# Two first parts on ScalarE before two second parts on VectorE, x's splits off GpSimd, and a new order in the fourth block

## The chip, the core and the metric

The kernel runs on one core of a Trainium2 chip. TensorE multiplies 128x128 tiles into PSUM; VectorE (DVE in the profile), ScalarE (ACT) and GpSimd (POOL) work on tiles of 128 partitions; SyncE (SP) issues the transfers to and from HBM. Each engine runs its own queue in order and waits on semaphores for the others. The metric is device time in microseconds (us); the median of the runs counts.

## The reference

One layer of a streaming encoder, for a prompt of 1024 frames and a second group of 64 new frames with caches. The part in which most of the change lies is the first projection and the two attentions behind it:

```python
h  = rms_norm(x, g_norm1)
p  = h @ w_in                       # q, k, v of 8 heads "A" and 8 heads "B", and forget logits
q, k = rms_norm(q, g_q), rms_norm(k, g_k)       # per head, 64 numbers
A: each chunk of 64 frames attends to itself and 8 chunks before, with a relative-position bias
B: causal attention, logit[t, s] += sum of log sigmoid(forget logit) over s < j <= t
x += concat(o_A, o_B) @ w_o
x += memory cross-attention (256 memory tokens, 4 heads);  x += ConvFFN(x)
```

## The kernel before, in words

**Split numbers.** TensorE multiplies in a rounded 32-bit format. For more exact results each operand is held as two parts: the first part is the operand rounded to that format, the second part is what rounding left. A product is then three matmuls (first x first, second x first, first x second: the names `hi` and `lo`). The split of x, `split_x` (L126), writes `xhi` on GpSimd for odd k and on ScalarE for even k (k counts eight slices of 128 of the 1024 model columns), then `xlo` on VectorE. The split of turned queries and keys, `gained` (L254), writes the first part on ScalarE and then the second on VectorE.

**The first stage** (0 to about 574 us) goes over eight pairs of heads, p = 0 to 7, and for each over eight blocks of 128 frames, t = 0 to 7, and the 64 new frames. A block's projection is 24 matmuls into a PSUM tile `pj` (two buffers). `proj` (L292) copies the result out on ScalarE (`qkraw`, `sq`, `vf`), and gives back two functions that are woven between the matmuls of later blocks:

- `norm`: the norms of queries and keys. VectorE sums and adds (`m`), splits the values (`v`); GpSimd takes the power (`r`) and scales (`qk`, `ko`).
- `turn`: TensorE transposes the four `qk` tiles into one PSUM bank `tq` (one buffer), and `gained` splits them twice: keys into `kh` and `kl`, queries into the two halves of `q`. The next block's transposes can't start before the bank has been read.

Scores then go to a PSUM tile `S` (one buffer), are read by VectorE (`mx`), put through the exponential on ScalarE, scaled on GpSimd, transposed (`PT`) and multiplied by the values (`O`).

**What pair 0 has besides.** In the first pair x itself must be split, 256 columns at a time (`columns(c, z)`: column group c, half z of the eight slices; c = 4 is the 64 new frames, in a tile `xs`), and its norms taken (`norms`: a square with a sum over each 128 rows on ScalarE, then `stats_end`). `early` says which of this work goes to which block, ahead of or behind the attention pieces of the block. `substeps(slow)` puts those pieces in a row: norms of the last block (`ns`), transposes held from the block before (`first`), scores, values. Blocks 0 and 1 of pair 0 are multiplied together; block 2 comes third, block 3 fourth.

**What sets the order.** The Python order is where a compile-time scheduler starts; it puts each engine's queue in an order by its own estimate of when things are ready. `in_order` pins part of it (the splits of x among it). So an edit in one place can move instructions elsewhere.

**The stage after** prepares keys and values of the memory: `load_mem` splits its 1024x256 input (`memT` into `mhi`, `mlo`, also with `gained`), `split_wm` the weights (`mwraw` into `mwhi`, `mwlo`), while the last attention pieces of the first stage are still running.

Of the kernel before, what the change touches and what calls it, by code (L numbers as in the profile page):

```python
# [9 lines left out]
ACT = mybir.ActivationFunctionType  # L10
ALU = mybir.AluOpType
# [30 lines left out]
def hybrid_step(ctx: ExitStack, tc: tile.TileContext, i: dict, o: dict):  # L42
# [3 lines left out]
    def f32(ap):  # L46
        return ap.bitcast(F32)
# [75 lines left out]
        e.tensor_tensor(lo[:, :nw], raw[:, :nw], f32(hi[:, :nw]), op=ALU.subtract)  # L123
        return hi, lo

    def split_x(hi, lo, raw, k):  # L126
        if k % 2:
            pool.tensor_scalar(hi, raw, gcol[:, 0, k:k + 1], 1.0, op0=ALU.mult, op1=ALU.mult)
        else:
            act.activation(hi, raw, ACT.Copy, scale=gcol[:, 0, k:k + 1])  # L130
        dve.scalar_tensor_tensor(lo, raw, gcol[:, 0, k:k + 1], f32(hi), op0=ALU.mult, op1=ALU.subtract)  # L131
# [40 lines left out]

    def split_col(c, k, raw):
        dst = [xs[:, k, a] for a in range(2)] if c == 4 else [a[:, k, c * 256:(c + 1) * 256] for a in x2]
        split_x(*dst, raw[:, k % 4], k)

    def columns(c, z, raw=None):
        raw = raw or load_x(c, z)
# [72 lines left out]
                           gk[:rows, kind:kind + 1].broadcast_to([rows, 2, 64]), op=ALU.mult)  # L251
        return qk, ko.rearrange("p h d -> p (h d)")

    def gained(hi, lo, src, g, rows=slice(0, P)):  # L254

        act.activation(hi, src, ACT.Copy, scale=g)
        dve.scalar_tensor_tensor(lo, src[rows], g[rows], f32(hi[rows]), op0=ALU.mult, op1=ALU.subtract)
# [34 lines left out]
    def proj(p, t, pj):  # L292

        g = groups.get((p, t // 2)) or Group()
        groups[p, t // 2] = g
        j = t % 2
        raw = wa.tile([P, 256], F32, name="qkraw", bufs=2)
        act.copy(raw, pj[:, 0:256])
        sq = squares(pj[:, 0:256], P)
        vf = wa.tile([P, 2, 64], F32, name="vf", bufs=2)  # L300
        act.activation(vf.rearrange("p h d -> p (h d)"), pj[:, 256:384], ACT.Copy, scale=rstd1[:, t:t + 1])
        if p == 0:
            dve.scalar_tensor_tensor(flog[:, t], pj[:, 384:392], rstd1[:, t:t + 1], bfb, op0=ALU.mult, op1=ALU.add)
        qk = kflat = None

        def norm():
            nonlocal qk, kflat
            qk, kflat = qk_norm(p, sq, raw, eps1[:, t:t + 1], P)
            dve.tensor_copy(g.v[:, j, :, 0], vf)
            dve.tensor_tensor(g.v[:, j, :, 1], vf, f32(g.v[:, j, :, 0]), op=ALU.subtract)  # L310

        def turn():
            tq = bank("tq").rearrange("p (a b) -> p a b", a=4)
            for h in range(4):
                pe.transpose(tq[:, h], qk[:, h].rearrange("p a d -> p (a d)"), ident)
            c = slice(j * P, j * P + P)
            kind = p // 4
            gained(g.kh[:, :, c], g.kl[:, :, c], tq[:, 2:4], gd[:, kind, 1:2])
            gained(g.q[:, :, c], g.q[64:, :, c], tq[:, 0:2], gd[:, kind, 0:1], slice(64, P))
            vflat = vf.rearrange("p h d -> p (h d)")  # L320
            cols = slice((p % 4) * P, (p % 4) * P + P)
            if p >= 4:
                nc.sync.dma_start(o["bk"][t * P:(t + 1) * P, cols], kflat)
                nc.sync.dma_start(o["bv"][t * P:(t + 1) * P, cols], vflat)
            elif t >= 4:
                nc.sync.dma_start(o["ak"][(t - 4) * P:(t - 3) * P, cols], kflat)
                nc.sync.dma_start(o["av"][(t - 4) * P:(t - 3) * P, cols], vflat)

        return norm, turn
# [229 lines left out]
    def substeps(slow=False):  # L559

        sc = todo[0].scores() if todo else []
        va = late.pop(0).values() if late else []
        if todo:
            late.append(todo.pop(0))
        ns, ts = [x for x, _ in turns], [x for _, x in turns]
        turns.clear()
        first = held[:]
        held[:] = ts if slow else []
        r = ns + first + sc[:1] + ends if slow else first + sc[:1] + ends + ns
        r += va[:1] + sc[1:] + va[1:-1] + ([] if slow else ts)  # L570
        ends[:] = va[-1:]
        return [f for f in r if f]
# [4 lines left out]
    def scale_gain():  # L577
# [1 line left out]

    early = {1: lambda: (norms(0, 1) + columns(1, 0, xraws[2]), []),  # L580
             2: lambda: (columns(1, 1, xraws[3]), [scale_gain] + norms(2, 3) + columns(2, 0, xraws[4]) + [lambda: load_bias(0)]),
             3: lambda: (columns(2, 1, xraws[5]), norms(4, 5)), 4: lambda: ([], columns(3, 0)), 5: lambda: ([], columns(3, 1) + norms(6)),
             6: lambda: ([], norms(7, 8) + columns(4, 0) + columns(4, 1))}
    forgetting = []
    for p, np_ in zip(PAIRS, PAIRS[1:] + (None,)):
# [56 lines left out]
    def load_mem(z):  # L642
        raw = wk.tile([P, N], F32, name="s", bufs=4)[:, :1024].rearrange("p (k t) -> p k t", k=4)
        nc.sync.dma_start(raw, i["memT"][4 * z:4 * z + 4].rearrange("k p t -> p k t"))
        for k in range(4):
            gained(mem[0][:, 4 * z + k], mem[1][:, 4 * z + k], raw[:, k], gcol[:, 3, 4 * z + k:4 * z + k + 1])

    def load_wm(n, z):
        raw = mp.tile([P, 4, 256], F32, name="mwraw", bufs=2)
# [54 lines left out]
    class Sample:  # L704
# [31 lines left out]
        def prep(self):  # L736
# [6 lines left out]
                pe.transpose(tq[:, x, :S], self.qd[:, x], ident[:S, :S])  # L743
            self.q = mq.tile([P, 2, S], F32R, name="sq_", bufs=2)
            self.kn = [mq.tile([P, 2, S], F32R, name=f"skn{x}", bufs=2) for x in range(2)]
            gained(self.q, self.q[64:], tq[:, 0:2, :S], gd[:, p // 4, 0:1], slice(64, P))
            gained(self.kn[0], self.kn[1], tq[:, 2:4, :S], gd[:, p // 4, 1:2])
            if p >= 4:
                b = self.s
                pool.tensor_scalar(b, b, stok[:, p - 4:p - 3], 1.0, op0=ALU.add, op1=ALU.mult)  # L750
# [1099 lines left out]
```

## Time and profile before

| | |
|---|---|
| median of 3 runs (lowest to highest) | 1797.08 us (1796.71 to 1797.51) |
| the profiled execution: its own time | 1797.27 us |
| its span in the trace | 1795.2 us |
| busy in the span: TensorE, VectorE, ScalarE, GpSimd | 1716.4, 1224.5, 930.2, 664.1 us |
| mean load of the DMA engines, 0 to 45 us and over the span | 0.76; 111 GB/s |

A row of a timeline reads: start in us, duration in us, engine, line, operation, output <- inputs, shape, how many alike in a row, and in brackets the idle time before it with what ended it. Matmuls overlap, so their durations are longer than their distance. A row of the waits reads: who waited, for whom, total us, how many times, the longest. A row of the windows reads: stretch, its length, then busy us of TensorE, its weight loads, VectorE, ScalarE and GpSimd with counts, then the granted TensorE clock, the DMA load and GB/s.

### The profile page before, as it was taken

The page shows a single profiled execution, that of the slowest core. Times are in us where ns is not written, and L with a number is a line of the kernel's source. Part 1 is how long each engine was busy: PE and PEld are TensorE (multiplying, and loading weights), DVE is VectorE, ACT ScalarE, POOL GpSimd, SP SyncE. Part 2 cuts the span into 40 slices and gives each one's busy share as a digit, 9 for nine tenths or more (in the row PEclk, how much of TensorE's full clock was granted, in tenths as well). Part 3 has the DMA queues.
Part 4 walks back from the last instruction along what each step waited for, and adds up shares of the span by engine and source line. Part 5 has one row for each costly group of instructions (what it writes and reads, how often), then busy time and mean ns, then how long its engine had stood idle before and what let it go on. Part 6 is the DMA issues. An engine that isn't in the chain of part 4 may idle for free. (4 is left out here: it accounts for less than half of the span.)

```text
span 1795.2 us, 34082 instructions
## 1 busy us (share of the span) xinstructions
PE 1716.4 (96%) x12432; PEld 1664.3 (93%) x12432; DVE 1224.5 (68%) x2710; ACT 930.2 (52%) x2042; POOL 664.1 (37%) x1025
## 2 busy tenths in 40 slices
PE   6898999999998888999999999999999999999999
PEld 5788999999997777999999999999999999999999
DVE  5778667677677797433444379877777777677994
ACT  5656667677677577433555455433333333434332
POOL 5656657779777554443444521100000000000000
PEclk8999999999999999999999999999999999999999
DMA  7322222122112776542111563222222222794232
GB/s 244 93 68 57 62 75 72 55 72 76 47 59 79 221 246 216 164 137 65 54 54 60 149 216 103 78 79 74 87 83 89 73 73 72 254 312 157 77 118 80
DMA packets 134248, 199.87 MB, mean 111 GB/s; under 512 B 20968, under 2 KB 74088, under 8 KB 134080
## 3 DMA queue, kind: packets, MB, share of 16 engines
q1 hardware_dynamic: 134080, 197.70, 34.8%
q8 instruction: 98, 1.61, 0.4%
q14 instruction: 70, 0.57, 0.1%
HBM read 155.35 MB, written 45.44 MB: 112 GB/s over the span
## 5 line engine op out<-in xcount | busy, mean ns | idle before, releaser
L288 PE MATMUL pj<-whi,xhi 128*128 128x384 f32 (+1 forms) x512 | 194.9, 381 | 3.4 <-ACT xhi L130 1.7
L288 PE MATMUL pj<-wlo,xhi 128*128 128x384 f32 (+1 forms) x512 | 176.1, 344 | 3.4 <-POOL wlo L123 3.4
L288 PE MATMUL pj<-whi,xlo 128*128 128x384 f32 (+1 forms) x512 | 174.7, 341 | 0.7 <-DVE xlo L131 0.7
L1540 POOL COPY s<-gp 128x2 f32<-128x2 f32 x22 | 15.8, 719 | 335.8 <-DVE gp L1539 335.8
L1434 PE MATMUL W<-h,hi 128*128 128x272 f32 x704 | 134.4, 288 | 1.4 <-ACT qlo L1570 1.4
L493 ACT ACTIVATE s<-s,mx 128x640 f32<-128x640 f32 (+7 forms) x128 | 94.4, 737 | 75.0 <-DVE mx L491 74.1
L1731 PE MATMUL W<-f,hi 128*128 128x272 f32 x672 | 127.7, 288 | 3.5 <-DVE f L1299 1.7
L530 DVE TENSOR_TENSOR ptl<-PT,pth 128x512 fp32r<-128x512 f32 (+2 forms) x192 | 99.5, 522 | 39.1 <-ACT pth L529 37.0
L1434 PEld LDWEIGHTS W<-h,hi 128*128 128x128 f32 x704 | 110.8, 188 | 1.7 <-ACT qlo L1570 1.6
L1731 PEld LDWEIGHTS W<-f,hi 128*128 128x128 f32 x672 | 105.3, 188 | 4.4 <-DVE gp L1505 2.4
L243 POOL TENSOR_TENSOR r<-m,mhalf 128x4 f32<-128x4 f32 (+1 forms) x72 | 73.9, 1027 | 92.4 <-DVE m L242 90.0
L529 ACT CAST pth<-PT 128x512 fp32r<-128x512 f32 (+2 forms) x192 | 85.0, 448 | 39.5 <-PE PT L528 37.9
L288 PEld LDWEIGHTS pj<-whi,xhi 128*128 128x128 f32 x512 | 98.9, 193 | 5.2 <-ACT xhi L130 2.3
L288 PEld LDWEIGHTS pj<-wlo,xhi 128*128 128x128 f32 x512 | 98.7, 193 | 5.3 <-POOL wlo L123 5.1
L1434 PE MATMUL W<-h,lo 128*128 128x272 f32 x352 | 101.8, 289 | 0.0
L1298 ACT CAST hi<-raw 128x512 fp32r<-128x512 f32 x68 | 42.2, 621 | 109.1 <-PE W L1434 59.1
L288 PEld LDWEIGHTS pj<-whi,xlo 128*128 128x128 f32 x512 | 97.3, 190 | 1.4 <-DVE xlo L131 1.2
L1731 PE MATMUL W<-f,lo 128*128 128x272 f32 x336 | 96.7, 288 | 0.0
L528 PE MATMUL PT<-ident,s 128*128 128x128 f32 x528 | 89.7, 277 | 6.2 <-DVE ptl L530 5.4
L246 POOL TENSOR_SCALAR qk<-qkraw,r 128x128 f32<-128x128 f32 x256 | 91.5, 375 | 5.9
L488 PE MATMUL S<-kh,q 128*128 128x256 f32 (+1 forms) x304 | 77.4, 280 | 12.8 <-DVE mx L491 12.7
L922 PE MATMUL pj<-a,hi 128*128 128x384 f32 (+1 forms) x352 | 89.5, 337 | 0.0
(606 smaller groups left out, 6051.3 us busy)
## 6 DMA issues: line engine op xcount, KB each, us to landing
raw<-in_w_down_dram SPq DMA_DIRECT2D x45, 256.0 KB, 2.9
wraw<-in_w_dram SPq DMA_DIRECT2D x56, 192.0 KB, 2.4
raw<-in_w_up_dram SPq DMA_DIRECT2D x41, 256.0 KB, 2.8
h<-ad SPq DMA_DIRECT2D x32, 272.0 KB, 4.7
mwraw<-in_w_mkv_dram SPq DMA_DIRECT2D x16, 512.0 KB, 5.2
raw<-in_w_mo_dram SPq DMA_DIRECT2D x32, 256.0 KB, 3.3
kvraw<-in_w_down_dram SPq DMA_DIRECT2D x32, 256.0 KB, 3.3
ad<-t SPq DMA_DIRECT2D x22, 272.0 KB, 2.1
```

The source lines that it names most:

```text
L243: pool.tensor_tensor(r[:rows], m[:rows], mhalf[:rows, 0:4], op=ALU.pow)
L246: pool.tensor_scalar(qk[:rows, h], raw[:rows, h * 64:(h + 1) * 64].rearrange("p (o d) -> p o d", o=1).broadcast_to([rows, 2, 64]), r[:rows ...
L288: pe.matmul(pj[:, :nw], x2[a][:, k, t * P:(t + 1) * P], wt[k][b][:, :nw], start=n == 0, stop=n == 3 * KT - 1)
L488: pe.matmul(sp[:, a:a + (k1 - k0) * P], q, kk[:, h, src], start=m == 0, stop=m == 1)
L493: act.activation(s[:, :n], s[:, :n], ACT.Exp, bias=mx, scale=-1.0, accum_out=sm)
L528: pe.transpose(pt[:, b - ch[0]], self.s[j][:, (b - w0) * P:(b - w0 + 1) * P], ident)
L529: act.copy(hi[:, f:f + n, j], pt[:, f:f + n])
L530: dve.tensor_tensor(lo[:, f:f + n, j], pt[:, f:f + n], f32(hi[:, f:f + n, j]), op=ALU.subtract)
L922: pe.matmul(out()[:, :cn], w[a][:, k % 4], x[b][k][:, c0:c0 + cn], start=k == 0 and n == 0, stop=k == KT - 1 and n == 2)
L1298: act.copy(hi, t)
L1434: pe.matmul(w[:, z, :Q], a(p, j), rights[j][b][:, z * Q:z * Q + Q], start=fresh and begin and j == 0 and x == 0, stop=final and end and j ...
L1731: pe.matmul(ws[m][:, z, :Q], la[p][:, m * P:(m + 1) * P], ra[b][:, z * Q:z * Q + Q], start=first and y == 0 and what in opening, stop=fina ...
```

## The change

```diff
-    def split_x(hi, lo, raw, k):
-        if k % 2:
+    def split_x(hi, lo, raw, k, first):
+        if k % 2 and first:
             pool.tensor_scalar(hi, raw, gcol[:, 0, k:k + 1], 1.0, op0=ALU.mult, op1=ALU.mult)
         else:
             act.activation(hi, raw, ACT.Copy, scale=gcol[:, 0, k:k + 1])
...
-        split_x(*dst, raw[:, k % 4], k)
+        split_x(*dst, raw[:, k % 4], k, c == 0)
...
-    def gained(hi, lo, src, g, rows=slice(0, P)):
-
-        act.activation(hi, src, ACT.Copy, scale=g)
-        dve.scalar_tensor_tensor(lo, src[rows], g[rows], f32(hi[rows]), op0=ALU.mult, op1=ALU.subtract)
+    def gained(*items):
+
+        for hi, lo, src, g, rows in items:
+            act.activation(hi, src, ACT.Copy, scale=g)
+        for hi, lo, src, g, rows in items:
+            dve.scalar_tensor_tensor(lo, src[rows], g[rows], f32(hi[rows]), op0=ALU.mult, op1=ALU.subtract)
...
-            gained(g.kh[:, :, c], g.kl[:, :, c], tq[:, 2:4], gd[:, kind, 1:2])
-            gained(g.q[:, :, c], g.q[64:, :, c], tq[:, 0:2], gd[:, kind, 0:1], slice(64, P))
+            gained((g.kh[:, :, c], g.kl[:, :, c], tq[:, 2:4], gd[:, kind, 1:2], ALL),
+                   (g.q[:, :, c], g.q[64:, :, c], tq[:, 0:2], gd[:, kind, 0:1], LOWER))
...
-        r = ns + first + sc[:1] + ends if slow else first + sc[:1] + ends + ns
+        r = first[:1] + ns + first[1:] + sc[:1] + ends if slow else first + sc[:1] + ends + ns
...
-             3: lambda: (columns(2, 1, xraws[5]), norms(4, 5)), 4: lambda: ([], columns(3, 0)), 5: lambda: ([], columns(3, 1) + norms(6)),
+             3: lambda: (columns(2, 1, xraws[5]) + norms(4, 5), []), 4: lambda: ([], columns(3, 0)), 5: lambda: ([], columns(3, 1) + norms(6)),
...
-                subs = ahead + subs + behind
+                subs = subs[:t == 3] + ahead + subs[t == 3:] + behind
```

It has four parts. `gained` takes both splits of one bank together (also for the new frames later; `load_mem` still calls it with one). The first parts of x are written by ScalarE except in column group 0. In blocks 2 to 6 of pair 0 the oldest held transposes go ahead of the norms. In the fourth block (t = 3) these transposes go ahead of the split of x, and the norms of x for blocks 4 and 5 come right behind that split instead of at the block's end. Behind `gained` the lines are numbered 4 higher.

**Fourth block, VectorE.** Before, from the logits of block 2 to the reduction of the first score (`m`, `v` are the norm of block 2; the two pairs `kl`, `q` are the transposes of blocks 0 and 1):

```order
L303 SCALAR_TENSOR_TENSOR flog<-pj,rstd_81,bfb 128x8
L131 SCALAR_TENSOR_TENSOR xlo<-ptl,gcol,xhi 128x256 x4
L241 TENSOR_REDUCE m<-sq 128x4
L242 TENSOR_SCALAR m<-m,eps_82 128x4
L309 CAST v<-vf 128x2x64
L310 TENSOR_TENSOR v<-vf,v 128x2x64
L257 SCALAR_TENSOR_TENSOR kl<-tq,gd,kh 128x2x128
L257 SCALAR_TENSOR_TENSOR q<-tq,gd,q 64x2x128
L257 SCALAR_TENSOR_TENSOR kl<-tq,gd,kh 128x2x128
L257 SCALAR_TENSOR_TENSOR q<-tq,gd,q 64x2x128
L491 ISA s,mx<-S,bias 128x128
```

Both pairs stand behind the split of x and block 2's norm. VectorE after, the same stretch (`ms_456`, `rsq_a`, `rstd_81`, `eps_82` end the norms of x for blocks 4 and 5):

```order
L259 SCALAR_TENSOR_TENSOR kl<-tq,gd,kh 128x2x128
L259 SCALAR_TENSOR_TENSOR q<-tq,gd,q 64x2x128
L131 SCALAR_TENSOR_TENSOR xlo<-ptl,gcol,xhi 128x256 x4
L159 TENSOR_SCALAR ms_456<-ssq 128x2
L78 TENSOR_TENSOR rsq_a<-ms_456,rsq_y 128x2
L79 SCALAR_TENSOR_TENSOR rsq_a<-rsq_a,rsq_y 128x2
L80 SCALAR_TENSOR_TENSOR rstd_81<-rsq_a,rsq_y 128x2
L161 TENSOR_SCALAR eps_82<-ms_456 128x2
L241 TENSOR_REDUCE m<-sq 128x4
L242 TENSOR_SCALAR m<-m,eps_82 128x4
L313 CAST v<-vf 128x2x64
L314 TENSOR_TENSOR v<-vf,v 128x2x64
```

Block 0's pair now stands ahead of the split of x; block 1's pair stands behind these rows, and with it the first score.

**Fourth block, ScalarE.** Before, from the end of block 2's projection (`vf`) on:

```order
L301 ACTIVATE vf<-pj,rstd_81 128x128
L130 ACTIVATE xhi<-ptl,gcol 128x256 x2
L256 ACTIVATE kh<-tq,gd 128x2x128
L256 ACTIVATE q<-tq,gd 128x2x128
L256 ACTIVATE kh<-tq,gd 128x2x128
L256 ACTIVATE q<-tq,gd 128x2x128
L493 ACTIVATE s,ssum<-s,mx 128x128
L493 ACTIVATE s,ssum<-s,mx 128x256
L154 ACTIVATE s,ssq<-s 128x1024 x2
L76 ACTIVATE rsq_y<-ms_508 128x2
```

Each `q` stands next to its `kh`, but had to wait for `kl` on VectorE in between. ScalarE after:

```order
L305 ACTIVATE vf<-pj,rstd_81 128x128
L257 ACTIVATE kh<-tq,gd 128x2x128
L257 ACTIVATE q<-tq,gd 128x2x128
L130 ACTIVATE xhi<-ptl,gcol 128x256 x4
L154 ACTIVATE s,ssq<-s 128x1024 x2
L76 ACTIVATE rsq_y<-ms_456 128x2
L77 ACTIVATE rsq_y<-rsq_y 128x2
L257 ACTIVATE kh<-tq,gd 128x2x128
L257 ACTIVATE q<-tq,gd 128x2x128
L497 ACTIVATE s,ssum<-s,mx 128x128
```

The two squares of x (L154), which wait for a transfer of `xn`, moved from behind the first scores to ahead of block 1's `kh` and `q`; the split of x has four instructions there, not two.

On TensorE the first transposes move ahead by three groups of three matmuls; the second ones now have two groups more ahead of them than before.

**Seventh block, GpSimd.** Before, around the first rows of `xs` (the new frames) and the norm of block 5 (`r`, `qk`):

```order
L496 TENSOR_SCALAR s<-s,ssum 128x512
L128 TENSOR_SCALAR xhi<-s,gcol 128x256 x2
L128 TENSOR_SCALAR xs<-s,gcol 128x64
L123 TENSOR_TENSOR wlo<-wraw,whi 128x384
L128 TENSOR_SCALAR xs<-s,gcol 128x64
L243 TENSOR_TENSOR r<-m,mhalf 128x4
L246 TENSOR_SCALAR qk<-qkraw,r 128x128 x4
L496 TENSOR_SCALAR s<-s,ssum 128x384
```

Two `xs`, which need a transfer, stand ahead of the norm. GpSimd after:

```order
L500 TENSOR_SCALAR s<-s,ssum 128x512
L500 TENSOR_SCALAR s<-s,ssum 128x384
L123 TENSOR_TENSOR wlo<-wraw,whi 128x384
L243 TENSOR_TENSOR r<-m,mhalf 128x4
L246 TENSOR_SCALAR qk<-qkraw,r 128x128 x4
```

The splits of x are gone from this queue (ScalarE has all eight `xs` in a row), and a scaling of scores moved ahead of the norm.

**Start of the stage after, VectorE.** Before, around the first memory splits:

```order
L241 TENSOR_REDUCE m<-sq 64x4
L242 TENSOR_SCALAR m<-m,eps_82 64x4
L257 SCALAR_TENSOR_TENSOR mlo<-s,gcol,mhi 128x256 x3
L658 TENSOR_TENSOR mwlo<-mwraw,mwhi 128x512
L553 TENSOR_TENSOR mix<-O,otmp 64x256
L491 ISA s,mx<-S,s 128x896
L491 ISA mx 128x1
L530 TENSOR_TENSOR ptl<-PT,pth 128x4x128
L257 SCALAR_TENSOR_TENSOR mlo<-s,gcol,mhi 128x256 x4
```

The score's reduction (L491) stands right behind the first pair's `mix`. VectorE after:

```order
L241 TENSOR_REDUCE m<-sq 64x4
L242 TENSOR_SCALAR m<-m,eps_82 64x4
L662 TENSOR_TENSOR mwlo<-mwraw,mwhi 128x512
L557 TENSOR_TENSOR mix<-O,otmp 64x256
L259 SCALAR_TENSOR_TENSOR mlo<-s,gcol,mhi 128x256 x4
L534 TENSOR_TENSOR ptl<-PT,pth 128x4x128 x2
L662 TENSOR_TENSOR mwlo<-mwraw,mwhi 128x512
L259 SCALAR_TENSOR_TENSOR mlo<-s,gcol,mhi 128x256 x4
L495 ISA s,mx<-S,s 128x896
```

The weight split `mwlo` goes ahead of the memory split `mlo`, and the reduction of a score (L495) falls behind eight `mlo`, two `ptl` and a second `mwlo`. The transfers moved likewise: on SyncE before,

```order
L644 DMA s<-in_memT_dram 128x4x256
L640 DMA gmk<-in_g_mk_dram 128x256
L650 DMA mwraw<-in_w_mkv_dram 128x1024 x2
L644 DMA s<-in_memT_dram 128x4x256
L358 DMA out_bk_dram<-ko 64x128
```

the memory's first half goes first; after, the first weights go ahead of it:

```order
L644 DMA gmk<-in_g_mk_dram 128x256
L654 DMA mwraw<-in_w_mkv_dram 128x1024
L648 DMA s<-in_memT_dram 128x4x256
L654 DMA mwraw<-in_w_mkv_dram 128x1024
L648 DMA s<-in_memT_dram 128x4x256
```

What both wait for stays the same; only which of the two lands first changed.

More of the change, by code (lines that the diff above doesn't have):

```diff
@@ L252, in qk_norm @@
         return qk, ko.rearrange("p h d -> p (h d)")
-    def gained(hi, lo, src, g, rows=slice(0, P)):
-        act.activation(hi, src, ACT.Copy, scale=g)
-        dve.scalar_tensor_tensor(lo, src[rows], g[rows], f32(hi[rows]), op0=ALU.mult, op1=ALU.subtract)
+    def gained(*items):
[3 more added lines that the diff above has]
+            dve.scalar_tensor_tensor(lo, src[rows], g[rows], f32(hi[rows]), op0=ALU.mult, op1=ALU.subtract)
+    ALL, LOWER = slice(0, P), slice(64, P)
     def pieces(n, size, one):
@@ L645, in load_mem @@
         for k in range(4):
-            gained(mem[0][:, 4 * z + k], mem[1][:, 4 * z + k], raw[:, k], gcol[:, 3, 4 * z + k:4 * z + k + 1])
+            gained((mem[0][:, 4 * z + k], mem[1][:, 4 * z + k], raw[:, k], gcol[:, 3, 4 * z + k:4 * z + k + 1], ALL))
     def load_wm(n, z):
@@ L745, in prep @@
             self.kn = [mq.tile([P, 2, S], F32R, name=f"skn{x}", bufs=2) for x in range(2)]
-            gained(self.q, self.q[64:], tq[:, 0:2, :S], gd[:, p // 4, 0:1], slice(64, P))
-            gained(self.kn[0], self.kn[1], tq[:, 2:4, :S], gd[:, p // 4, 1:2])
+            gained((self.q, self.q[64:], tq[:, 0:2, :S], gd[:, p // 4, 0:1], LOWER),
+                   (self.kn[0], self.kn[1], tq[:, 2:4, :S], gd[:, p // 4, 1:2], ALL))
             if p >= 4:
```

## The prediction

> **What bounds the kernel now.** I read the page first, then the windows, the waits of TensorE, and the timelines of all queues where TensorE waits.
>
> ```profile
> PE 1716.4 (96%) x12432; PEld 1664.3 (93%) x12432; DVE 1224.5 (68%) x2710; ACT 930.2 (52%) x2042; POOL 664.1 (37%) x1025
> 0.00:45.00 45.00, 29.34 (x138) 26.09 (x139) 23.64 (x72) 22.60 (x54) 22.62 (x42) 0.89 0.76 244
> 45.00:90.00 45.00, 37.29 (x235) 34.35 (x234) 34.52 (x112) 30.49 (x86) 28.45 (x52) 0.96 0.32 93
> 90.00:540.00 450.00, 436.15 (x2992) 415.80 (x2991) 322.04 (x899) 303.03 (x783) 317.40 (x569) 1.00 0.22 64
> 540.00:720.00 180.00, 151.44 (x1031) 134.01 (x1030) 141.07 (x339) 122.05 (x298) 99.66 (x126) 0.95 0.62 194
> 720.00:1795.00 1075.00, 1062.13 (x8044) 1054.03 (x8042) 703.20 (x1291) 452.05 (x823) 195.96 (x239) 1.00 0.35 112
> ACT q L256 <- DVE kl L257: 20.0, 21, 6.3
> PE tq L315 <- POOL qk L246: 9.6, 2, 8.6
> ```
>
> TensorE is the bound: what it idles is all there is to win, 15.7 us up to 45 (45.00 less 29.34), 7.7 up to 90, 13.9 in the 450 us of the other seven pairs, 28.6 from 540 to 720. ScalarE's 20.0 us of waiting for `kl` are not TensorE's. So the places that count are the blocks of pair 0 and the change of stage. TensorE there:
>
> ```profile
> 20.98 0.45 PE L288 MATMUL pj<-whi,xhi 128*128 128x392 f32 x1 [1.69 <-DVE flog L303]
> 28.28 0.34 PE L288 MATMUL pj<-whi,xlo 128*128 128x392 f32 x1
> 37.23 1.09 PE L315 MATMUL tq<-ident,qk 128*128 128x128 f32 x4 [8.61 <-POOL qk L246]
> 40.85 0.55 PE L488 MATMUL S<-kh,q 128*128 128x256 f32 x1 [1.13 <-DVE mx L491]
> 43.38 0.51 PE L288 MATMUL pj<-whi,xhi 128*128 128x392 f32 x1
> 49.40 0.38 PE L488 MATMUL S<-kh,q 128*128 128x256 f32 x1 [2.76 <-DVE mx L491]
> 50.74 0.53 PE L288 MATMUL pj<-wlo,xhi 128*128 128x392 f32 x1
> 70.98 1.52 PE L315 MATMUL tq<-ident,qk 128*128 128x128 f32 x4 [0.97 <-POOL qk L246]
> 78.71 0.30 PE L488 MATMUL S<-kh,q 128*128 128x128 f32 x1 [1.02 <-DVE mx L491]
> 582.52 0.55 PE L543 MATMUL O<-pth,v 128*128 128x256 f32 x1 [7.67 <-DVE mix L553]
> 588.64 0.58 PE L488 MATMUL S<-kh,q 128*128 128x256 f32 x1 [0.24 <-DVE mx L491]
> ```
>
> The 8.61 us before block 1's transposes are put down to `qk`, but these wait for the bank `tq` as well, and the other queues say that it was the bank:
>
> ```profile
> 23.31 1.02 POOL L243 TENSOR_TENSOR r<-m,mhalf 128x4 f32<-128x4 f32 x1 [2.80 <-DVE m L242]
> 24.44 1.52 POOL L246 TENSOR_SCALAR qk<-qkraw,r 128x128 f32<-128x128 f32 x4
> 27.58 1.70 POOL L246 TENSOR_SCALAR qk<-qkraw,r 128x128 f32<-128x128 f32 x4
> 30.31 1.92 DVE L131 SCALAR_TENSOR_TENSOR xlo<-pth,gcol,xhi 128x256 fp32r<-128x256 f32 x3 [2.22 <-POOL xhi L128]
> 35.58 0.48 DVE L257 SCALAR_TENSOR_TENSOR kl<-tq,gd,kh 128x256 fp32r<-128x256 f32 x1
> 26.95 0.89 ACT L130 ACTIVATE xhi<-pth,gcol 128x256 fp32r<-128x256 f32 x2
> 36.09 0.47 ACT L256 ACTIVATE q<-tq,gd 128x256 fp32r<-128x256 f32 x1 [6.29 <-DVE kl L257]
> 38.35 0.47 ACT L256 ACTIVATE kh<-tq,gd 128x256 fp32r<-128x256 f32 x1 [1.79 <-PE tq L315]
> 38.86 0.48 DVE L257 SCALAR_TENSOR_TENSOR kl<-tq,gd,kh 128x256 fp32r<-128x256 f32 x1 [1.78 <-ACT kh L256]
> 39.38 0.47 ACT L256 ACTIVATE q<-tq,gd 128x256 fp32r<-128x256 f32 x1 [0.55 <-DVE kl L257]
> 39.89 0.49 DVE L257 SCALAR_TENSOR_TENSOR q<-tq,gd,q 64x256 fp32r<-64x256 f32 x1 [0.54 <-ACT q L256]
> 42.64 1.04 ACT L154 ACTIVATE s<-s 128x1024 f32<-128x1024 f32 x1
> 30.81 0.91 SPq L147 DMA_DIRECT2D s<-in_xn_dram  x2
> s<-in_xn_dram SPq DMA_DIRECT2D x2, 512.0 KB, 6.0
> ```
>
> Block 1's `qk` is there at 29.3 (27.58 + 1.70); the bank is free only after 36.09, since `kl` stood on VectorE behind splits of x that waited for GpSimd, which was still at the norms.
>
> **The change, part by part.** Durations are from these rows; I replay the fourth block on their clock.
>
> *First transposes.* A half of x's split is now four `xhi` on ScalarE, 4 x 0.45 = 1.8 us for 0.89. That is hidden behind the second block's matmuls, but VectorE's `xlo` follow it, and block 0's norm with them: +0.7, so `qk` ends at 26.7 (24.44 + 1.52 + 0.7). The matmuls of block 2 start some 0.4 earlier than 20.98, since `flog` waits less behind `xlo`; 27 matmuls at 0.18 apart bring TensorE to the moved transposes at 25.4. New wait: 1.3.
>
> *Second transposes.* Eighteen matmuls, to 30.2. ScalarE: four `xhi` from 26.95, the copies of block 2 (0.8), `kh` and `q` together (0.9), done at 30.3; `kl` and `q` on VectorE 0.95, done at 31.2. Transposes at 31.2, not 37.23, with six more matmuls done. Were this the end of it, 7 us would be won.
>
> *What is late next.* Block 1's `kh` now stands behind the second half of x (1.8) and two squares (1.04 each, 0.2 more to read the sum) that wait for `xn`. The pair of transfers landed 6.0 us after issue at 31.3, at 37.3. Now the first goes ahead of a pair of bias transfers, the second leaves at 30.8: in 4 to 6 us, the earlier in what the DMA engines have idle (0.76 up to 45), so 34.8 to 36.8, I take 35.6. Square, inverse root over ScalarE and VectorE (0.75), `kh` and `q`: 38.5. VectorE: rest of the root, the norm of block 2 (1.35), the pair: 40.5, reduction 0.35: the second score starts at 40.9, where it did (40.85). TensorE waits from 32.2: the gap of 8.6 has moved, not gone. But the fourth block then has six matmuls fewer to go, at the slow distance of 0.33 that stands behind a gap: the fifth starts at 41.7, not 43.38. **Gain 1.7** (none if `xn` lands at 37.3, 2.7 at 34.6).
>
> *Fifth block.* From the second score to the next wait were 8.55 us (40.85 to 49.40), with both squares in it (42.64). Now: exponential, second reduction, exponential, copies, pair of splits, pair, norm, reduction: 6.2 us, to 47.1. **Gain 2.3 in all.** The wait of 2.76 shrinks to 0.5 to 1.5, and the slow matmuls behind it (0.53 long, eleven from 50.74, 0.15 more each) go: **1.6**. Both ends: 0 and 1.6; I take 1.6, since shorter waits than 2 us show no slow rows behind them (70.98, 78.71).
>
> *Sixth block.* ScalarE has two more `xhi` (0.9) ahead of the copies that everything waits for, and the norm now waits for the pair of splits on VectorE. **Loss 1.5** (0 to 2).
>
> *Seventh and eighth.*
>
> ```profile
> 67.58 0.34 POOL L128 TENSOR_SCALAR xs<-s,gcol 128x64 fp32r<-128x64 f32 x1 [3.56 <-DMA s<-in_xT_dram]
> 73.43 1.98 DVE L131 SCALAR_TENSOR_TENSOR xs<-s,gcol,xs 128x64 fp32r<-128x64 f32 x3 [1.59 <-POOL xs L128]
> ```
>
> GpSimd stood at `xs` for 3.56 us ahead of block 5's norm, and VectorE 1.59 for the last `xs`; both waits leave with `xs`, and with them TensorE's 0.97 and 1.02. **Gain 2.0** (0 to 2.9, with the stretched transposes of 70.98).
>
> *All other turned keys and queries.* Four rows above alternate strictly, 2.03 us from 38.35 to 40.38. The Trainium skill (PSUM — Partial Sum Buffer, PSUM bank collisions raise a hardware error) says two engines may not read one bank at once; the trace agrees. By that rule `kl` must now wait for both ScalarE parts, 0.9 + 0.95 = 1.85 us: only 0.2 shorter, and `kl` itself 0.4 later. If reads could overlap it would be 1.4, and my three turns 1.2 us better. The sum goes by the alternating rows, so by 1.85. In the other pairs TensorE idles 13.9 us over 450, little of it at a bank: **0** (-2 to +2, since the scheduler moved other rows too).
>
> *Change of stage.*
>
> ```profile
> 574.23 0.51 ACT L256 ACTIVATE mhi<-s,gcol 128x256 fp32r<-128x256 f32 x1 [0.58 <-DMA s<-in_memT_dram]
> 577.84 1.14 ACT L657 CAST mwhi<-mwraw 128x512 fp32r<-128x512 f32 x2 [1.30 <-DMA mwraw<-in_w_mkv_dram]
> 579.00 2.92 DVE L658 TENSOR_TENSOR mwlo<-mwraw,mwhi 128x512 fp32r<-128x512 f32 x1 [1.96 <-ACT mwhi L657]
> 582.30 1.07 DVE L491 CUSTOM_DVE_ANT_0 s<-S,s 128x896 f32<-128x896 f32 x1
> 583.91 1.66 DVE L257 SCALAR_TENSOR_TENSOR mlo<-s,gcol,mhi 128x256 fp32r<-128x256 f32 x4
> ```
>
> TensorE's 7.67 us ended with `mix`, behind `mwlo`, behind `mwhi`, behind the weights. These are now issued first and land some 2.5 us sooner (as `memT`, first before, was there at 574.2 and the weights at 577.8, one transfer between): -2.5 to -3.9 for the first `O`. The reduction behind it falls after eight `mlo` (3.3) and more, to about 585, so the score before 588.64 starts at 587.6: **gain 1.0** (3 gained to 3 lost).
>
> Sum: 3.9 (1.7, 0.6 of the fifth block beyond it, 1.6), less 1.5, plus 2.0, plus 1.0 = 5.4 us. The profiled execution took 1797.27 us, 2.07 over its span, 0.19 over the median. From 1797.27: 1791.9; from the median 1791.7. I say 1791.8. Behind 720 us nothing moves: TensorE is busy 1062 of 1075 us and everything follows it.
>
> **The rivals.**
>
> *The gap only moves.* `xn` lands at 37.3 (fourth block 0, so 1.7 less), the wait before the fifth block's score stays over 2 us and with it the slow rows (1.6 less). 5.4 - 3.3 = 2.1: 1795.2, no change to be measured. For it: the same bytes stand ahead of the second `xn`. The Trainium skill (TensorE: Matmul & The Clock Gate, What's actually happening) gives a free-running window of some 3.4 us after which an idle TensorE runs at half rate; the 0.53 us matmuls from 50.74, behind 2.76 us of idle, agree with half rate, and by that rule the moved gap stays slow behind it, as I count. Against it: squares leave the fifth block whatever lands when.
>
> *The change of stage costs.* The weights land no sooner, the first `O` starts at 582.5, and the reduction stands behind 8 `mlo`, 2 `ptl` and `mwlo` (3.3 + 1.3 + 1.3 = 5.9 us) with nothing for TensorE that isn't bound to the one score buffer: +5.9, and the start gives the fourth block's 1.7 alone: 4.2 slower, 1801.3. It decides once it costs more than pair 0 gives. For it: `mwlo` took 2.92 us beside a busy GpSimd. Against: eight `O` and three transposes moved ahead of the score.
>
> *More.* `xn` at 34.6 (1.0), nothing lost in the sixth block (1.5), the change of stage 3 (2.0): 5.4 + 4.5 = 9.9, 1787.2.
>
> **How the numbers follow.** Within 0.2%, 3.6 us, is what a measurement here can't tell from no change. Forecast 1788.5 to 1793.5: 0.50. The gap only moves: 0.26. The change of stage costs: 0.12. More: 0.12. Faster by over 0.2%: 0.50 and 0.12, 0.62; the same 0.26; slower 0.12. The range takes in the first, second and most of the last, and half of what lies between no change and the slow rival: 1786.8 to 1799.0.
>
> **What would show it.** After: no wait of 8 us before the second transposes, but about 1.3 before the first and 7 to 9 before the second score, behind L154. No ScalarE `q` waiting for `kl`. In the fifth block a wait of at most 1.5 before the score and no slow matmuls from then on. No GpSimd row of `xs`. The first `O` of the change of stage near 579 on the shifted clock. I am wrong if the squares don't wait for `xn`, if TensorE's wait before the scores stays over 2 us in the fifth block, or if the score at the change of stage is the later one.

## The result, and the profile after

The changed kernel takes 1817.74 us (1815.32 to 1819.19), the kernel before 1797.30 on the same chip: 20.4 us slower, a ratio of 1.0113 with an interval of 1.0095 to 1.0130. The forecast was 1791.8, its range ended at 1799.0. The profiled execution has a span of 1816.2 us, 21.0 more than before's.

First the page's line of engines, then the windows of the same stretches as before (stretch, length, busy TensorE, its weight loads, VectorE, ScalarE, GpSimd, granted clock, DMA load, GB/s), then TensorE's longest waits:

```profile
PE 1728.8 (95%) x12432; PEld 1672.2 (92%) x12432; DVE 1234.6 (68%) x2710; ACT 931.7 (51%) x2058; POOL 664.3 (37%) x1009
0.00:45.00 45.00, 30.51 (x139) 27.00 (x140) 24.07 (x77) 27.68 (x69) 18.13 (x34) 0.84 0.79 255
45.00:90.00 45.00, 40.27 (x227) 35.67 (x226) 33.26 (x107) 30.36 (x87) 24.86 (x44) 0.90 0.28 81
90.00:540.00 450.00, 430.31 (x2943) 408.05 (x2942) 324.21 (x875) 293.90 (x767) 317.31 (x561) 1.00 0.22 64
540.00:720.00 180.00, 152.11 (x1023) 136.62 (x1022) 133.47 (x326) 112.28 (x281) 97.92 (x126) 0.91 0.55 172
PE S L492 <- DVE mx L495: 17.8, 6, 9.3
PE O L547 <- ACT pth L533: 10.8, 7, 7.7
PE pj L292 <- POOL wlo L123: 8.4, 7, 2.0
```

The same three waits before:

```profile
PE S L488 <- DVE mx L491: 12.7, 14, 2.8
PE O L543 <- DVE mix L553: 7.7, 1, 7.7
PE pj L288 <- POOL wlo L123: 3.4, 6, 0.9
```

The loss isn't in pair 0, on which most of the prediction was spent. In the windows it stands where the prediction put a zero: 90 to 540 us, 2943 matmuls done where before did 2992, and in the change of stage behind it. The wait for `wlo` grew from 3.4 to 8.4 us. Of the 17.8 us of `S`, 9.3 are the moved gap of pair 0, which the prediction expected, and 5.08 at the change of stage are new. The 7.7 us ahead of an `O` were there before too, with another row ending them.

How late the changed kernel is at a place is read best from the same matmul in both traces. The median difference around some places of before's clock, in us (negative: earlier than before):

| at | 53 | 62 | 95 | 200 | 260 | 330 | 545 | 605 | 735 | 1700 |
|---|---|---|---|---|---|---|---|---|---|---|
| changed | -3.4 | -0.8 | +0.7 | +3.1 | +5.3 | +6.9 | +9.2 | +16.2 | +18.8 | +21.1 |

Three things are seen: pair 0 wins 3.4 us up to its fifth block and has lost them at its end; then come steps of about 2 at 171, 239 and 308 us, the ends of pairs 1, 2 and 3; then one of 7 between 545 and 605.

A trace is one execution, so small differences in this table are soft. Eight kernels of this document have the whole change in pair 0 (changed, e3, e5 to e10): at 53 us they are 2.9 to 5.3 us ahead of before, at 140 us they stand anywhere from 2.1 ahead to 2.3 behind. Runs with before's queues behind 605 us (e2, e3, e4, e14 to e16) lost 0.2 to 2.1 us from 605 to 735 and 0.1 to 3.3 from there to 1700, so the changed kernel's 2.6 and 2.3 there may be mostly scatter. Where the order of rows differs, near 62, the median moves by more than 1 us with the rows chosen.

**The ends of the pairs.** At 239 us of the changed kernel and 237 of before, GpSimd and TensorE; first before, then after (`r`, `qk`, `ko` with 64 rows are the norm of the new frames, `wlo` the second part of the next pair's weights):

```profile
231.70 1.01 POOL L243 TENSOR_TENSOR r<-m,mhalf 64x4 f32<-64x4 f32 x1 [1.61 <-DVE m L242]
232.69 1.00 POOL L123 TENSOR_TENSOR wlo<-wraw,whi 128x384 fp32r<-128x384 f32 x1
233.68 2.01 POOL L246 TENSOR_SCALAR qk<-sm,r 64x128 f32<-64x128 f32 x4
236.18 0.99 POOL L123 TENSOR_TENSOR wlo<-wraw,whi 128x384 fp32r<-128x384 f32 x1
237.23 0.44 PE L288 MATMUL pj<-wlo,xhi 128*128 128x384 f32 x1 [0.85 <-POOL wlo L123]
```

```profile
234.70 1.01 POOL L243 TENSOR_TENSOR r<-m,mhalf 64x4 f32<-64x4 f32 x1 [1.30 <-DVE m L242]
235.81 1.77 POOL L246 TENSOR_SCALAR qk<-sm,r 64x128 f32<-64x128 f32 x4
237.66 0.45 POOL L250 TENSOR_TENSOR ko<-qk,gk 64x128 f32<-64x128 f32 x1
238.08 1.95 POOL L123 TENSOR_TENSOR wlo<-wraw,whi 128x384 fp32r<-128x384 f32 x2
234.83 1.33 ACT L121 CAST whi<-wraw 128x384 fp32r<-128x384 f32 x3
239.12 0.45 PE L292 MATMUL pj<-wlo,xhi 128*128 128x384 f32 x1 [2.02 <-POOL wlo L123]
```

Before, one `wlo` goes between `r` and `qk`, and TensorE waits for the second; after, both stand behind four `qk` and `ko`, whose results nothing on TensorE needs there, and TensorE waits for the first. The first `whi` was done at 235.3, so `wlo` could have run at 235.8; it ran at 238.1.

**The change of stage.** After: TensorE, then VectorE. Everything here goes through one score buffer, which the reduction of `S` (L495) frees, and this comes 9.2 us behind `mix`:

```profile
591.76 0.58 PE L547 MATMUL O<-pth,v 128*128 128x256 f32 x1 [7.66 <-ACT pth L533]
600.60 0.58 PE L492 MATMUL S<-kh,q 128*128 128x256 f32 x1 [5.08 <-DVE mx L495]
589.88 0.41 DVE L557 TENSOR_TENSOR mix<-O,otmp 64x256 f32<-64x256 f32 x1
590.21 1.65 DVE L259 SCALAR_TENSOR_TENSOR mlo<-s,gcol,mhi 128x256 fp32r<-128x256 f32 x4
591.79 1.27 DVE L534 TENSOR_TENSOR ptl<-PT,pth 128x512 fp32r<-128x512 f32 x2
592.99 2.78 DVE L662 TENSOR_TENSOR mwlo<-mwraw,mwhi 128x512 fp32r<-128x512 f32 x1
595.69 3.84 DVE L259 SCALAR_TENSOR_TENSOR mlo<-s,gcol,mhi 128x256 fp32r<-128x256 f32 x4
599.46 1.08 DVE L495 CUSTOM_DVE_ANT_0 s<-S,s 128x896 f32<-128x896 f32 x1
```

Before, the reduction stood right behind `mix`:

```profile
581.96 0.42 DVE L553 TENSOR_TENSOR mix<-O,otmp 64x256 f32<-64x256 f32 x1
582.30 1.07 DVE L491 CUSTOM_DVE_ANT_0 s<-S,s 128x896 f32<-128x896 f32 x1
```

The transfers didn't come sooner either: the weights are issued at 581.6 and their `mwhi` starts at 587.4, since the queue of transfers waited for a store of `ko`. The transposes just ahead of this place start 9.25 us later than before (583.04 and 573.79), `mwhi` 9.6 us later (587.44 and 577.84): the weights are 0.4 us late, not early. ScalarE and VectorE stood idle for them (3.1 and 3.9 us), where before they split the memory's first half in that time. The first `O` starts 9.24 us later than before (591.76 and 582.52), so up to there nothing is lost or won; the loss comes behind it.

### The profile page after: what moved, and what is told of

Its sections match the earlier page's. It is cut to its first block, busy times and chain, and to the rows that moved or that the text cites. A ratio compares the mean times of both kernels' runs of the same rounds, so it can differ in the third digit from the quotient of the medians.

```text
span 1816.2 us, 34154 instructions
## 1 busy us (share of the span) xinstructions
PE 1728.8 (95%) x12432; PEld 1672.2 (92%) x12432; DVE 1234.6 (68%) x2710; ACT 931.7 (51%) x2058; POOL 664.3 (37%) x1009
## 4 chain that ended last, share of the span: by engine, by line
PE 54%; DVE 2%; DMA 2%; issue 1%; POOL 1%; ACT 1%; SPq 0%; POOLq 0%; DVEq 0%; ACTq 0%
PE W L1438 25%; PE pj L926 11%; PE W L1735 11%; PE W L926 1%; PE S L1181 1%; PE pj L672 1%; POOL lo L909 1%; PE tq L1217 1%; PE O L1217 1%; DMA raw<-in_w_down_dram 0%; PE O L827 0%; PE PT L1204 0%; DMA kvraw<-in_w_down_dram 0%; PE PT L926 0%; DMA h<-ad 0%
## 5 line engine op out<-in xcount | busy, mean ns | idle before, releaser
L492 PE MATMUL S<-kh,q 128*128 128x256 f32 (+1 forms) x304 | 78.3, 282 | 17.9 <-DVE mx L495 17.8
L500 POOL TENSOR_SCALAR s<-s,ssum 128x640 f32<-128x640 f32 (+6 forms) x96 | 71.3, 743 | 54.9 <-DVE ssum L498 50.8
```

The lines of the kernel that those rows point to most:

```text
L492: pe.matmul(sp[:, a:a + (k1 - k0) * P], q, kk[:, h, src], start=m == 0, stop=m == 1)
L500: pool.tensor_scalar(s[:, :n], s[:, :n], sm, 1.0, op0=ALU.mult, op1=ALU.mult)
```

## The experiments

Each was timed against the kernel before on its chip. The difference to before is what follows in the table; the changed kernel's is +20.4.

| run | what it is | us (median) | ratio, interval |
|---|---|---|---|
| e1 | before with the pairing alone | +23.5 | 1.0124 (1.0109 to 1.0139) |
| e2 | changed without the pairing | -0.1 | 1.0003 (0.9995 to 1.0012) |
| e3 | changed, pairing in pair 0 only | +1.2 | 1.0006 (0.9996 to 1.0017) |
| e4 | before with x's parts on ScalarE alone | -1.9 | 0.9991 (0.9982 to 0.9999) |
| e5 | changed, pairing not in blocks 6, 7 of pairs 1 to 7 | +5.1 | 1.0036 (1.0022 to 1.0049) |
| e6 | changed, no pairing in pair 7 | +14.9 | 1.0084 (1.0070 to 1.0098) |
| e7 | changed, memory loaded before weights | +15.5 | 1.0084 (1.0070 to 1.0098) |
| e8 | changed, `wlo` ahead of `qk` | +11.3 | 1.0058 (1.0046 to 1.0071) |
| e9 | e6 and no pairing for the new frames | +14.0 | 1.0070 (1.0057 to 1.0082) |
| e10 | e9 and `wlo` ahead of `qk` | +5.6 | 1.0026 (1.0015 to 1.0037) |
| e11 | e4 and `wlo` ahead of `qk` | -0.6 | 0.9994 (0.9985 to 1.0003) |
| e12 | e11 and memory weights split later | +1.1 | 1.0009 (1.0000 to 1.0018) |
| e13 | before, `qk` ahead of `wlo`, no pairing | +4.3 | 1.0031 (1.0019 to 1.0042) |
| e14 | e4 and pairing in pair 0 | -1.3 | 0.9995 (0.9986 to 1.0004) |
| e15 | before with the turn's place alone | +2.5 | 1.0012 (1.0002 to 1.0022) |
| e16 | before with the fourth block's order alone | +3.5 | 1.0019 (1.0010 to 1.0027) |

**Which part loses (e1 to e4).** The four parts of the diff, taken alone or left out. e1 has only this of it:

```diff
-            gained(g.kh[:, :, c], g.kl[:, :, c], tq[:, 2:4], gd[:, kind, 1:2])
-            gained(g.q[:, :, c], g.q[64:, :, c], tq[:, 0:2], gd[:, kind, 0:1], slice(64, P))
+            gained((g.kh[:, :, c], g.kl[:, :, c], tq[:, 2:4], gd[:, kind, 1:2], ALL),
+                   (g.q[:, :, c], g.q[64:, :, c], tq[:, 0:2], gd[:, kind, 0:1], LOWER))
```

e2 calls it once for each item, e3 does so for `p > 0` only, e4 keeps only `split_x`.

> The kernel before with the pairing in gained alone (in all eight pairs of heads); x's split, the turns' place and the fourth block as before. Behind pair 0 its queues are those of the changed kernel. Theory 1 (the loss comes from the order that the scheduler makes of the pairing in pairs 1 to 7 and at the change of stage: 8.2 us over the pairs, 10 at the change of stage, 2.3 near 1640 us): slower than before by 16 to 20 us. Theory 2 (the loss needs x's first parts on ScalarE or the new order of the fourth block): slower by less than 5 us.

> The changed kernel with the pairing taken out (each bank read first part, second part, first part, second part as before); x's split, the turns' place and the fourth block as changed. Behind pair 0 its queues are those of before. Theory 1: within 3 us of before, since 18 of the 20 us are gone and pair 0 gave the changed kernel nothing net. Theory 2: slower by 15 us or more.

> The changed kernel with the pairing kept in pair 0 alone; the seven other pairs and the new frames read a bank as before, and their queues are in the order of before. Theory 1: what is left is pair 0 alone, which in the changed kernel ends 0.5 us later than before: 1796 to 1799 us. Theory 3 (each paired read costs by itself, a little per block, in pair 0 as elsewhere): the same here, so this run tells only what pair 0 is worth; if it is 3 us or more faster than before, pair 0 did give what was forecast.

> The kernel before with x's first parts on ScalarE (column groups 1 to 4) and nothing else. The prediction put 2.0 us of gain on the xs rows leaving GpSimd, and 1.5 of loss on ScalarE in the sixth block. If both are right: faster by 0.5 to 2 us. If ScalarE is the later one in pair 0: slower by 0.5 to 2.

Theory 1 holds: the pairing alone makes the whole loss (23.5 us, more than the 16 to 20 expected), and without it, or with it in pair 0 only, the rest of the change is worth nothing that can be measured (e3's 1799.52 lies 0.5 above its range, its interval includes no change). Theory 2 is out. x's split alone is the one part that wins, 1.9 us; in its trace TensorE is 3.9 ahead at the end of pair 0 and gives 2.4 of it back between 545 and 735 us.

**Where (e5, e6, e7).** Edits: in `turn`, `both` stands for the two items,

```diff
+            for x in ([both] if p == 0 or t < 6 else [both[:1], both[1:]]):     # e5; in e6: if p < 7
+                gained(*x)
```

and in e7 two lines change places, `load_mem(0)` ahead of `load_wm(0, 0)`.

> The changed kernel with the pairing in pair 0 and, in pairs 1 to 7, in blocks 0 to 5 only (blocks 6 and 7 and the new frames read part by part as before). With it GpSimd has the second weight part ahead of the new frames' qk again at the end of a pair, and the change of stage loads memT first again. Theory 1a (the loss lies in two places, the ends of the pairs and the change of stage, where the order turned over): 1796 to 1801 us, although 36 + 6 of the paired reads are kept. Theory 3 (each paired read costs by itself, since kl comes 0.4 us later): it keeps three quarters of the paired reads, so 1808 us or more.

> The changed kernel with the pairing in pairs 0 to 6, not in pair 7. The ends of the pairs stay as changed, the change of stage has the queues of before (memT's first half before the weights, mlo before mwlo, the score's reduction right behind mix). Theory 1a: the 7 to 10 us of the change of stage go, the 8 of the ends of pairs stay: 1805 to 1811 us. Theory 3: one eighth of the loss goes, 1815 us.

> The changed kernel with one line moved: at the change of stage the memory's first half is loaded ahead of the first weights (load_mem(0) before load_wm(0, 0)). All else of the change stays, the paired reads in pair 7 too. Theory 1a, with the order of the two loads as the cause at that place: 7 to 10 us less than the changed kernel, 1807 to 1811 us. If the change of stage is late for another reason (the norm of the new frames or the paired reads of pair 7 themselves): within 3 us of the changed kernel.

e5 keeps 50 of the prompt's 64 paired reads and loses 5 us of 20: so it is mostly not the reads, though it is 2 above what theory 1a allowed. In its trace TensorE stands against before as it did at 140 us until 605 (-2.1 and -1.8); what it loses comes after. e6 gives 5.5 back, less than the 7 to 10 expected. Its trace shows it at the change of stage: the step from 545 to 605 is 1.2, not 7.0, though from 605 to 735 it loses 4.9, where the changed kernel lost 2.6. The reduction again follows `mix`:

```profile
589.71 0.42 DVE L559 TENSOR_TENSOR mix<-O,otmp 64x256 f32<-64x256 f32 x1
590.05 1.07 DVE L497 CUSTOM_DVE_ANT_0 s<-S,s 128x896 f32<-128x896 f32 x1
591.18 0.58 PE L494 MATMUL S<-kh,q 128*128 128x256 f32 x1 [0.36 <-DVE mx L497]
```

e7 gives 4.9, less than the 7 to 10 expected, and its trace shows only 2.2 of it at the change of stage (a step of 4.8, not 7.0). So the order of the two loads is a part of the cause there. With the reduction the next row behind `mix` again, three things are still late: both loads are issued behind the store of `ko`, from 581.8 on; TensorE waits 8.53 us for `mix`; and the reduction then waits for GpSimd, which prepares its bias:

```profile
593.67 1.09 DVE L495 CUSTOM_DVE_ANT_0 s<-S,s 128x896 f32<-128x896 f32 x1 [1.08 <-POOL s L479]
```

No run moves the reduction alone, so what each row costs at this place is argued from the traces, not shown.

**The row order itself (e8, e13).** e8 leaves the paired reads and adds a dependence of order:

```diff
+        if n in new_qk and wlo:          # the new frames' four qk, behind the last wlo on GpSimd
+            tc.add_manual_dep(ins, wlo, ...)
```

e13 has no paired read, and calls the new frames' `norm()` ahead of the fifth weight split for `p in (1, 2, 3)`, which puts both `wlo` behind `qk` and `ko`.

> The changed kernel with the new frames' four qk scalings on GpSimd held behind the weights' last second part (wlo) of that pair's end. TensorE, VectorE and ScalarE have the changed kernel's queues row for row; on GpSimd wlo goes ahead of qk at six ends of pairs. Theory 1a: TensorE's waits for wlo at 171, 239 and 308 us (1.66, 2.02, 2.05) go, and the short waits for ptl behind them (0.58, 0.23 each): 5 to 8 us less than the changed kernel, 1809 to 1813 us; the three later ends, with a wait of 0.81 as before, give 0 to 1 each. Rival: the paired reads make scores late there, and wlo is only what ends last: under 2 us less.

> The kernel before, no bank read in pairs, with the new frames' norm written ahead of the weights' fifth split at the ends of pairs 1, 2 and 3, so that GpSimd has r, four qk, ko and only then the two wlo there, as in the changed kernel. ScalarE's queue is that of before row for row; TensorE has the three products of that weight 13 rows later. Theory 1 (this row order alone costs, pairing or not): TensorE waits for wlo 1 to 2 us longer at each of the three ends: 1800 to 1804 us, less than the changed kernel's 7 because the scheduler saw the lateness and moved the products. Theory 3 (the order costs nothing, the paired read is what is late): 1797 to 1799 us.

TensorE's waits for `wlo` at the ends of pairs 1 to 3, in the stretch from 140 us to 320 or 325 (before, changed, e13; in e8 there is none):

```profile
PE pj L288 <- POOL wlo L123: 2.6, 3, 0.9
PE pj L292 <- POOL wlo L123: 5.7, 3, 2.0
PE pj L292 <- POOL wlo L123: 5.4, 3, 1.9
```

e8 gives 9.1 us back, some more than expected, and its trace stays level from 140 to 330 us (0.0 and -0.2) where the changed kernel lost 6.7. e13 loses 4.3 without one paired read: in its trace 5.2 us between 140 and 330. The order of a few rows on GpSimd (four `qk` and `ko` ahead of `wlo`) is what costs; the pairing is what made the scheduler choose it.

The price isn't the waiting alone. In e13 the wait for `wlo` grew by 2.8 us over the three ends, as in the changed kernel (3.1). But behind two of them TensorE then ran slow for about 3 us, its products of 384 columns 0.52 us long and not 0.34; behind the changed kernel's own waits it didn't. The 3 us behind the wait at the second end, first in e13, then in the changed kernel:

```profile
237.00:240.00 3.00, 3.00 (x14) 3.00 (x14) 1.01 (x4) 0.90 (x4) 0.80 (x1) 0.51 0.30 96
240.00:243.00 3.00, 2.27 (x15) 1.69 (x13) 3.00 (x6) 0.89 (x2) 0.81 (x2) 1.00 0.45 115
```

The granted clock is 0.51 behind a wait of 1.87 us and 1.00 behind one of 2.02: the length of the wait doesn't decide it. In the changed kernel, waits for `ptl` behind that for `wlo` take part of the loss instead (2.8 us, before 0.3); in e8 they are still there (2.5) and cost nothing that the trace shows.

**What the paired reads cost themselves (e9, e10).** e9 also calls `gained` once for each item in the new frames' `prep`; e10 adds e8's dependence.

> As the run without the pairing in pair 7, and the attention of the new frames (prep, behind 600 us) reads its bank part by part too. From the change of stage on every queue is that of before; the ends of pairs stay as changed. Theory 1b (the pairing of the new frames turns the order over a third time, between 600 and 750 us, and this is why the run without the pairing in pair 7 kept 7 us there): 1804 to 1808 us, 4 to 7 less than that run. Theory 1a (two places only, and the 7 us are the scatter of transfers in that stretch): 1810 to 1814 us.

> The run before this one with, besides, the new frames' qk held behind the weights' second part at the ends of pairs. Of the paired reads those of pairs 0 to 6 are kept, 56 of the 64 of the prompt. Theory 1 (order only): within 3 us of before, 1796 to 1801 us. Theory 3 (each paired read costs by itself, 0.3 us and more): 56 of them would leave 10 us or more, 1808 us or more.

Theory 1b falls: e9 is no faster than e6 as timed (1812.66 and 1812.55), so the new frames' pairing is no third place. e10 keeps 56 paired reads and loses 5.6 us, between the two theories. Its trace, of an execution 1.8 us slower than its median, has 2.3 us before 140, within the scatter of pair 0; 1.5 between 140 and 545, about 0.03 us for each of the 48 paired reads of pairs 1 to 6; nothing at the change of stage; and 5.4 behind 605, of which 4.2 up to 735. What these are stays open: runs with before's queues there (e2, e3, e15, e16) lost 0.2 to 2.1 us up to 735, half as much at most.

**Versions that might beat both (e11, e12, e14), and the parts of pair 0 (e15, e16).** e12 writes the first two `split_wm` one step later. e14 is e4 and `both` for `p == 0`. e15 keeps only `first[:1] + ns + first[1:]`, e16 only the lines for t = 3.

> The kernel before with x's first parts on ScalarE and the new frames' qk behind the weights' second part; nothing else of the change. If both act where they did so far: x's split 1.9 us, and TensorE's three waits of 0.85 us for wlo, 2.6 us: 1792 to 1795 us against 1797.5. If the second part of the weights was not what ended last there: 1796 us.

> The run before this one with, besides, the memory weights' first splits written one step later at the change of stage, so that ScalarE copies otmp and pth, and VectorE takes mix, ptl and the score's reduction, ahead of the splits that wait for the weights' transfer. If that wait is what holds TensorE for 7.67 us from 574.8: it goes on at about 577 to 578, 4 to 5 us less, of which the stage behind may take some back: 1788 to 1793 us. If the memory's products then wait for the later weights as long: no gain or a loss of up to 4.

> The kernel before with x's first parts on ScalarE and the paired reads in pair 0 alone; the turns' place and the fourth block as before. TensorE's queue is that of before but for five rows of pair 0. If paired reads are a gain where the bank is waited for (the second transposes waited 8.61 us for it): 1794 to 1796 us, better than x's split alone (1.9 us faster than before). If they only put ScalarE's other rows later: 1797 to 1800 us.

> The kernel before with the oldest held transposes ahead of the norms in blocks 2 to 6 of pair 0, and nothing else. The prediction gave the earlier second transposes nothing by themselves, since the wait moves to the second score: within 2 us of before. If the wait of 8.6 us went with it: 4 us faster.

> The kernel before with the fourth block's order alone (norms of x for blocks 4 and 5 right behind the split of x). The prediction counted on squares leaving the fifth block (2.3 us in all, and 1.6 for its slow matmuls): faster by 2 to 4 us if that holds by itself. If the squares stand in the way of block 1's keys and the wait of 8.6 us only stands elsewhere: within 1.5 us of before, or slower.

e11 took the waits for `wlo` away and won nothing: in the same stretch TensorE now waits for `ptl`, 3.1 us where before had 0.3 (before first):

```profile
PE PT L528 <- DVE ptl L530: 0.3, 1, 0.3
PE PT L535 <- DVE ptl L537: 3.1, 6, 0.8
```

So `wlo` ended last in the changed kernel, and only as one of two in the kernel before. e12 cut the wait of 7.67 us to 3.17 and is no faster: the stage behind gave it back, among others in a new wait of 3.8 us for the first part of a later weight. e14 is 1.3 faster, inside the noise; in its trace it ends pair 0 about as far ahead as e4 (4.2 and 3.9 us). e15 and e16 lose 2.5 and 3.5: neither pays for itself, and the fourth block's order alone is slower, as the second half of its expectation had it, with a wait of 11.5 us ahead of the second transposes: block 0's `kh` stands behind the two squares, the second of which starts at 36.3, and with it the bank. The only version whose interval lies wholly below no change is e4, by 0.1% at the median; e11 and e14, which contain it, don't confirm it.

## Why the prediction was wrong

By its steps, with the changed kernel's TensorE and ScalarE rows in pair 0:

```profile
24.94 1.37 PE L319 MATMUL tq<-ident,qk 128*128 128x128 f32 x4
30.79 0.63 PE L319 MATMUL tq<-ident,qk 128*128 128x128 f32 x4 [1.25 <-ACT xhi L130]
36.52 1.06 ACT L154 ACTIVATE s<-s 128x1024 f32<-128x1024 f32 x1 [2.36 <-DMA s<-in_xn_dram]
41.53 0.55 PE L492 MATMUL S<-kh,q 128*128 128x256 f32 x1 [9.35 <-DVE mx L495]
47.59 0.39 PE L492 MATMUL S<-kh,q 128*128 128x256 f32 x1
56.69 1.52 PE L319 MATMUL tq<-ident,qk 128*128 128x128 f32 x4 [1.55 <-POOL qk L246]
60.27 0.53 PE L292 MATMUL pj<-whi,xlo 128*128 128x392 f32 x1
70.77 1.75 PE L319 MATMUL tq<-ident,qk 128*128 128x128 f32 x4 [1.57 <-POOL qk L246]
72.64 0.53 PE L292 MATMUL pj<-wlo,xhi 128*128 128x392 f32 x1
```

- *First and second transposes:* the new wait of 1.3 is there (1.25), ahead of the second instead of the first; the second start at 30.79, forecast 31.2. Right, but for the place of the small wait.
- *What is late next, fifth block:* the wait of 7 to 9 us ahead of the second score, behind the squares, is 9.35, and the score starts at 41.53 (40.9), the fifth block's at 47.59 (47.1) with no wait. TensorE is 3.4 us ahead at 53; forecast 3.9. Right.
- *Sixth block:* loss about 2.6 (3.4 ahead to 0.8), forecast 1.5, behind a wait of 1.55 for `qk`. Mis-sized. Of it some 1.4 us, an estimate from the rows from 57.86 to 61.13 against the same rows before, are slow matmuls behind that wait (0.53 us long, not 0.34). The prediction had counted them out: shorter waits than 2 us, it said, show no slow rows behind them. Here they do.
- *Seventh and eighth:* forecast a gain of 2.0, lost 1.4. The wait at 70.77 didn't go, though `xs` did: the norm on GpSimd now stood behind a `wlo`, done at 69.03, and VectorE's `m`, done at 69.05. Slow matmuls stand behind this wait too, up to 74.7, some 1.1 us by the same estimate. With x's split alone (e4) the gain was there, 1.5 us. A term that is right for its part and wrong in company.
- *All other turned keys and queries, 0:* the step that failed. By itself a paired read costs next to nothing, as forecast, but the term was sized by the read and not by the queues that the scheduler made of it: 8.5 us from 95 to 545 in the trace. With the one dependence of e8, 1.4 us are left there; as timed it is worth 9.1 us. The text named the risk ("the scheduler moved other rows too") and gave it 2 us. The order of GpSimd at the ends of pairs was to be had before the result, and its price too: `wlo` had already been what TensorE waited for there (0.85 us, three times), so what was put ahead of it counted nearly in full: at 239 us the first `wlo` ran 2.3 us later than it could have, and the step there is about 2.
- *Change of stage, a gain of 1.0:* wrong in sign. The second rival, a chance of 0.12 and a price of 5.9, is what happened: the reduction behind eight `mlo`, two `ptl` and `mwlo`, 9.2 us from `mix` to the reduction, and the weights no sooner; the first `O`, forecast 2.5 to 3.9 us sooner, came when it had. It cost 5.5 us as timed (e6), 7.0 in the trace, and the last of the three signs of being wrong, the score that is the later one, is the one that came true. The argument against it, eight `O` and three transposes ahead of the score, was true and covered 3.7 us. The argument for the gain took the weights' place in the queue of transfers for their time of landing; but what stood ahead of the queue, a store of the last block's `ko`, had moved too.

The sum: 9.1 for the ends of pairs, 5.5 to 6.4 for the change of stage (e6, e9), 5.6 left with both mended (e10), together 20.2 to 21.1, where 20.4 was measured. The first two are causes shown by taking them out; the 5.6 are not explained.

## What to carry to other kernels

Where a compile-time scheduler orders the queues, the cost of an edit is not the cost of its rows: compare every engine's new order first at each place where the trace already shows the bounding engine waiting, even briefly, and price what now stands ahead of the row it waits for. A wait that is under a microsecond in the old profile marks a row with no slack. Here rows put ahead of it cost about their full length, while taking the wait away won nothing, since another was right behind. And a change with several parts is worth timing part by part: here one part carried the loss, one a small gain.

## What the chip showed beside this

- *Two reads of a bank.* Two ScalarE reads in a row start 0.36 us apart though each is 0.47 long, and VectorE's first follows only when the second is done:

```profile
28.72 0.47 ACT L257 ACTIVATE kh<-tq,gd 128x256 fp32r<-128x256 f32 x1
29.08 0.48 ACT L257 ACTIVATE q<-tq,gd 128x256 fp32r<-128x256 f32 x1
29.66 0.47 DVE L259 SCALAR_TENSOR_TENSOR kl<-tq,gd,kh 128x256 fp32r<-128x256 f32 x1
30.15 0.49 DVE L259 SCALAR_TENSOR_TENSOR q<-tq,gd,q 64x256 fp32r<-64x256 f32 x1
```

  The four take 1.92 us, 0.11 less than the alternating four before (2.03).
- *VectorE beside GpSimd.* The `mwlo` of 2.78 us above ran while GpSimd wrote a bias tile and did its own `mwlo`; four `mlo` took 3.84 us in such company. At 590.21 four took only 1.65, but then three of GpSimd's `qk` took 3.06 us, where four had taken 1.40 before. With GpSimd idle, at 604.04, a `mwlo` took 0.67. The Trainium skill (SBUF — State Buffer, Who interferes with whom) says that a VectorE instruction with two inputs in SBUF contends with a GpSimd instruction that reads SBUF; the trace agrees.
- *Slow matmuls.* Behind the two gaps of 7.66 and 5.08 us, matmuls of 256 columns take 0.41 us instead of 0.28 for most of 591.8 to 610, and the granted clock of 540 to 720 us is 0.91, before 0.95. Short waits between them seem to keep TensorE slow; this was not tested.
